# A two-layer hybrid decoder trunk in float32 on one core: rotary tables advanced inside the value phases and gate paths, head 0's values one step later, the last row tile in two column groups

## The chip, the cores and the metric

The kernel runs on one core of a Trainium2 chip. The metric is the device time of one execution in microseconds; the median of three runs is 2310.65 us. Five engines work side by side, each through its own queue in order: TensorE (PE, with its weight loads shown as PEld), VectorE (DVE), ScalarE (ACT), GpSimd (POOL) and SyncE (SP), which here issues the DMA transfers. An instruction waits for others by semaphores, and whatever stands behind a waiting instruction in its queue waits too.

## The reference

Two layers, then a final RMSNorm. Sequence 1024, width 1024, batch 1, everything in float32.

```python
for l in range(DEPTH):
    shift, scale, gate = jnp.split(c_act @ w_ada[l] + b_ada[l], 3, axis=-1)
    h = rmsnorm(x, norm_g[l]) * (1.0 + scale[:, None, :]) + shift[:, None, :]
    p = h @ w_in[l]
    mq, mk, mv, mo, mz, mi, mf, rq, rk, rv, rz = split_cols(p)
    qk = jax.nn.silu(causal_dwconv(jnp.concatenate([mq, mk], axis=-1), conv_w[l], conv_b[l]))
    ...
    y_m = jax.nn.sigmoid(mo) * head_layernorm(cell, gn_m[l], N_HEADS_MLSTM) * jax.nn.silu(mz)
    rq_h = rotary(rq.reshape(B, S, N_HEADS_RET, HD_R), positions)
    rk_h = rotary(rk.reshape(B, S, N_HEADS_RET, HD_R), positions)
    ret = retention_chunkwise(rq_h, rk_h, rv.reshape(B, S, N_HEADS_RET, HD_R))
    y_r = head_layernorm(ret, gn_r[l], N_HEADS_RET) * jax.nn.silu(rz)
    y = jnp.concatenate([y_m, y_r], axis=-1) @ w_out[l]
    x = x + gate[:, None, :] * y
return rmsnorm(x, final_g)
```

`cell` is the output of a chunkwise mLSTM with four heads of 256 columns, `ret` that of a chunkwise retention with four more. The rotary tables are cos and sin of position times 128 frequencies; they depend on the positions alone and are the same for both layers and for all retention heads.

## The kernel before

**Products.** Every float32 operand of a product is split into a rounded high part and a remainder (`split_to`, L620: the high part is cast on ACT in L621, the remainder subtracted in L622 on POOL or, where the caller says so, on DVE). `mm3` (L144) makes a product of three matmuls, high by high, high by low, low by high; its lines L145 to L147 carry most of TensorE's time.

**Heads.** The loop at L1268 goes over eight head groups, called heads 0 to 7 here: 0 to 3 are mLSTM, 4 to 7 retention. For a head come, in this order, the gate path (z and o columns, `gate_path`), the q and k columns (`qk_ml` with a convolution `conv_silu`, L630 to L645, or `qk_ret` with the rotary tables), the v columns (`v_path`, with the split of the values `v_split`, L596), and the attention. Columns of z, o, q and k are made by `proj_units`: a column block of 128 is two halves of 512 positions, each half two steps of 12 matmuls with 512 columns; after the second step `evac` empties the PSUM bank. `v_path` makes four chunks of two steps, each step 24 matmuls with 256 columns. PSUM has four banks under the tag `pp` for these products and four under `pa` for attention.

**Steps.** `run_units` (L140) calls `tick` after each step of such a generator. `tick` counts a clock and lets every generator that was put aside by `launch(gen, delay)` run on when it is due; `yield n` puts it off by n steps. So the attention of a head is written out in pieces between the projection steps of the heads after it. `attention` (L743) makes scores (L774), state updates (L807), values (L829) and their normalisation (L871) chunk by chunk; a state update runs from a product over L825 (cf, on DVE) to the cast cH (ACT, L621) and the remainder cL (DVE, L622), which the next values product (L845) needs. Head 0's attention is launched at the end of its turn with a delay of two steps (L1293), and so runs beside head 1's gate, q and k columns; those of heads 1 to 3 are launched ahead of their v columns with a delay of 7 or 4 (L1287).

**Order.** TensorE's instructions stand in the order in which the program writes them (L1107). For the start (L1109 to L1245) that holds for all engines. Everywhere else a scheduler decides the order on DVE, ACT, POOL and SP, and may draw an instruction that waits for little ahead of others that are written before it.

**Rotary tables.** `rotary_tables` (L374) makes the tables of the angle in four quarters of 256 positions. A quarter loads the positions by DMA (L381), needs 26 operations on DVE with 256 columns (L383 to L407) on three tiles of the tag `g`, and stores two results in DRAM (L410). The tag `g` has six buffers, which the z and o products of the gate path (L549 to L561) use too. In this kernel the generator is launched after head 1 of layer 0 with a delay of 14 steps (L1300). Head 3's attention loads the tables at its end (`load_rotary`, L735).

**Output product.** `out_units` (L975) multiplies the gated values by W_out. In the last layer a bank is a tile of 128 rows by 512 columns, and for the last half and the last 512 columns the final four of sixteen pieces are done row tile by row tile (`alone` is 4). `row_evac` (L1025) then loads the residual in four DMAs (L1030), multiplies by the gate (L1032), adds (L1033) and sums the squares on ACT (L1034); `final_rows` (L1090) turns the sum into a root (L1093, and L1094 on POOL) and `final_scale` (L1081) scales and stores the row (L1085, L1087, L1088).

Of the kernel before, what the change touches and what calls it, by code (L numbers as in the profile page):

```python
# [11 lines left out]
F32 = mybir.dt.float32  # L12
# [3 lines left out]
ALU = mybir.AluOpType  # L16
# [64 lines left out]
def tile_hybrid_trunk(ctx, tc, x, xt, c, positions, w_ada, b_ada, norm_g, w_in, conv_w, conv_b,  # L81
# [16 lines left out]
    def nm(s):  # L98
        uid[0] += 1
        return f"{s}_{uid[0]}"  # L100
# [39 lines left out]
    def run_units(gen):  # L140
        for _ in gen:
            tick()
# [231 lines left out]
    def rotary_tables():  # L374
        c1, c2, c3 = two_pi_split()
        tiles = [wt("g", 512, 6) for _ in range(3)]
        ang, turn, tmp, rnd, a1, pos = (t[:, i * CH:(i + 1) * CH] for t in tiles for i in range(2))
        a2 = ang
        for n in range(4):
            i, cs = n // 2, slice((n % 2) * CH, (n % 2 + 1) * CH)  # L380
            Q.dma_start(pos.bitcast(I32), positions[0:1, n * CH:(n + 1) * CH].to_broadcast([P, CH]))  # L381
            yield 2
            V.tensor_copy(ang, pos.bitcast(I32))  # L383
            V.tensor_scalar(ang, ang, kc[:, C_FREQ:C_FREQ + 1], None, ALU.mult)
            V.tensor_copy(a1.bitcast(F32R), ang)
            yield 1
            V.tensor_tensor(a2, ang, a1, ALU.subtract)
            V.tensor_scalar(turn, a1, c3, None, ALU.mult)
            yield 1
            V.scalar_tensor_tensor(turn, a2, c3, turn, ALU.mult, ALU.add)  # L390
            V.scalar_tensor_tensor(turn, a2, c2, turn, ALU.mult, ALU.add)
            yield 1
            for src, cc in ((a1, c2), (a2, c1), (a1, c1)):
                V.tensor_scalar(tmp, src, cc, None, ALU.mult)
                V.tensor_scalar(rnd, tmp, MAG_I, -MAG_I, ALU.add, ALU.add)
                yield 1
                V.tensor_tensor(tmp, tmp, rnd, ALU.subtract)
                V.tensor_tensor(turn, turn, tmp, ALU.add)
                yield 1
            parts = ((1, 0.0, tmp), (0, 0.25, a1))  # L400
            for which, sh, dst in parts:
                if sh:
                    V.tensor_scalar(turn, turn, sh, None, ALU.add)
                V.tensor_scalar(rnd, turn, MAG_I, -MAG_I, ALU.add, ALU.add)
                V.tensor_tensor(dst, turn, rnd, ALU.subtract)
                yield 1
                V.tensor_scalar(dst, dst, 0.49999994, -0.49999994, ALU.min, ALU.max)  # L407
            yield 2
            for which, sh, dst in parts:
                Q.dma_start(rdr[which][i][:, cs], dst)  # L410
            yield 2

    def v0_gates(l):
        gr = wt("wgr", KT * 8, 1)
# [328 lines left out]
    def attention(l, hg, gt, qT, kT, kt, vs, gp, rot):  # L743
# [230 lines left out]

    def out_units(l, half, cc, loads, evac, alone=0):  # L975
        banks = [ps_a() if cc else ps_p() for _ in range(4)]

        def product(k, piece, i):
            y, w = piece
            if l == 0:  # L980
                cs = slice(i * P, (i + 1) * P)
                mm3(banks[i], (w[0][:, cs], w[1][:, cs]), y, k == 0, k == 15)
            else:
                ts = slice(i * P, (i + 1) * P)
                mm3(banks[i], (y[0][:, ts], y[1][:, ts]), w, k == 0, k == 15)

        together = 16 - alone
        for k in range(together):
            piece = loads.take()
            for i in range(4):  # L990
                product(k, piece, i)
            yield
        pieces = [loads.take() for _ in range(alone)]
        for i in range(4):
            for k in range(together, 16):
                product(k, pieces[k - together], i)
            evac(half, cc, i, banks[i])
            if alone:
                yield

# [24 lines left out]
    def row_evac(gb, xnew, ss, done=None):  # L1025
        def evac(half, cc, tt, bank):
            xr = bt()
            src = xdr[half].rearrange("(g i) (b j) -> b i g j", i=32, j=32)[:, :, cc * 16:(cc + 1) * 16, :]
            for b in range(4):
                Q.dma_start(xr[b * 32:(b + 1) * 32, :].rearrange("i (g j) -> i g j", j=32), src[4 * tt + b])  # L1030
            tmp = wt("th", 512, 5)
            V.tensor_tensor(tmp, bank, gb[cc], ALU.mult)  # L1032
            V.tensor_tensor(xr, xr, tmp, ALU.add)  # L1033
            A.activation(tmp, xr, AF.Square, accum_out=ss[:, tt, cc:cc + 1])  # L1034
# [55 lines left out]
    def final_rows(xn, ss, half, fg, rows):  # L1090
        for tt in rows:
            s, rs = (cst.tile([P, 4], F32, tag=t, bufs=2, name=nm(t))[:, 0:1] for t in ("nrm", "nrmr"))
            V.tensor_scalar(s, ss[:, tt, 0:1], ss[:, tt, 1:2], EPS * D, ALU.add, ALU.add)  # L1093
            G.tensor_tensor(rs, s, mhalf[:, 0:1], ALU.pow)  # L1094
            final_scale(xn, rs, tt, half, fg)

    def final_later(xn, ss, half, fg):
        for tt in range(4):
            yield 2
            final_rows(xn, ss, half, fg, (tt,))  # L1100

    def gains_later(xn, fg):
        for tt in range(4):
# [57 lines left out]
    for l in range(DEPTH):  # L1161
# [103 lines left out]
        run_units(proj_units(load_w(w_in[l], zcol(1, 0), P), hT, z_evac(gp1, 0)))  # L1265
        gb = []
        gcol = gsh[0][:, 0, :]
        for hg in range(8):  # L1268
            ml = hg < 4
            if hg == 0:  # L1270
                rot = [[], []]
            if hg > 0:
                gp = gp1 if hg == 1 else [[None, None], [None, None]]
                run_units(gate_path(l, hg, hT, gp, 0, 1 if hg == 7 else 2, hg > 1))
            vs = []
            kt = [None] * NCH
            kT = [[None, None], [None, None]]
            qT = [[None] * NCH, [None] * NCH]
            if hg == 4:
                run_units(v_path(l, hg, hT, gt, vs))  # L1280
            for which, res in ((0, qT), (1, kT)):
                if ml:
                    run_units(qk_ml(l, hg, which, hT, gt, kt, res))
                else:
                    run_units(qk_ret(l, hg % 4, which, hT, kt, res, *rot))
            if 0 < hg < 4:
                launch(attention(l, hg, gt, qT, kT, kt, vs, gp, rot), 4 if hg == 3 else 7)  # L1287
            if hg not in (0, 4):
# [24 lines left out]
        for half in range(2):  # L1313
            if l < DEPTH - 1:
                xn, sq = [None] * KT, bt()
                keep = keep_rows(half, xn)
                evac = column_evac(gcol, xn, sq, keep)
                run_units(out_units(l, half, 0, loads, evac))
                run_units(out_units(l, half, 1, loads, evac, 2 if half else 0))
                launch(norm_later(l + 1, xn, sq, nhT, half, keep, (1, 2, 0) if half else (3, 3, 11)))  # L1320
                continue
            xn = [[None, None] for _ in range(4)]
            ss = new_ss()
            run_units(out_units(l, half, 0, loads, row_evac(gb, xn, ss)))
# [37 lines left out]
```

## Time and profile before

| | |
|---|---|
| median of three runs | 2310.65 us (2310.61 to 2311.62) |
| the profiled execution | 2310.2 us, of which the span from first to last instruction is 2308.5 us |
| matmuls | 12415 |
| mean granted TensorE clock | 0.997 |
| HBM read, written | 201.57 MB, 55.61 MB |

The profile is that of one execution. A row of its timeline has the start in us from the span's beginning, the duration in us, the engine, the line of the kernel, the operation, what it writes and reads (`out<-in`, buffer numbers left out), shapes, how many instructions were merged, and in brackets the idle time of the engine before it with what ended that wait. Matmuls are pipelined: one with 256 columns is shown with 0.28 us but the next starts about 0.12 us later. Idle time of an engine that is not the bottleneck costs nothing by itself.

### The profile page before, as it was taken

The page shows a single profiled execution, that of the slowest core. Times are in us where ns is not written, and L with a number is a line of the kernel's source. Part 1 is how long each engine was busy: PE and PEld are TensorE (multiplying, and loading weights), DVE is VectorE, ACT ScalarE, POOL GpSimd, SP SyncE. Part 2 cuts the span into 40 slices and gives each one's busy share as a digit, 9 for nine tenths or more (in the row PEclk, how much of TensorE's full clock was granted, in tenths as well). Part 3 has the DMA queues.
Part 4 walks back from the last instruction along what each step waited for, and adds up shares of the span by engine and source line. Part 5 has one row for each costly group of instructions (what it writes and reads, how often), then busy time and mean ns, then how long its engine had stood idle before and what let it go on. Part 6 is the DMA issues. An engine that isn't in the chain of part 4 may idle for free.

```text
span 2308.5 us, 34327 instructions
## 1 busy us (share of the span) xinstructions
PE 2273.0 (98%) x12415; PEld 1956.8 (85%) x12415; DVE 1337.9 (58%) x2823; ACT 919.3 (40%) x1768; POOL 830.7 (36%) x823
## 2 busy tenths in 40 slices
PE   7999999899999999999999999999999999999998
PEld 5888888789988888988888889888898888988886
DVE  7477669656555555585435676555563545557562
ACT  5535443444332323343544444344443323234342
POOL 1343433333244334224563433233334334341313
PEclk9999999999999999999999999999999999999999
DMA  8223233324433533385532323322223233436674
GB/s 257 80 64 96 74 80 85 78 74 117 119 100 102 149 94 83 113 261 201 174 107 70 81 72 81 82 74 74 75 71 94 76 91 88 124 81 212 182 240 120
DMA packets 360247, 259.45 MB, mean 112 GB/s; under 512 B 113267, under 2 KB 297339, under 8 KB 360077
## 3 DMA queue, kind: packets, MB, share of 16 engines
q1 hardware_dynamic: 360076, 257.26, 39.3%
q8 instruction: 97, 1.59, 0.3%
q14 instruction: 74, 0.60, 0.1%
HBM read 201.57 MB, written 55.61 MB: 111 GB/s over the span
## 4 chain that ended last, share of the span: by engine, by line
PE 91%; DVE 4%; DMA 2%; issue 1%; ACT 1%; POOL 0%; SPq 0%; POOLq 0%; ACTq 0%; DVEq 0%
PE pp L145 23%; PE pp L146 23%; PE pp L147 23%; PE pa L147 5%; PE pa L146 5%; PE pa L145 5%; PE pa L845 3%; PE pa L772 2%; DMA b<-in_w_ada_dram 1%; DVE acc L639 1%; DMA b<-in_x_dram 1%; PE pp L1178 0%; PE pp L1181 0%; PE pp L1179 0%; DVE acc L644 0%
## 5 line engine op out<-in xcount | busy, mean ns | idle before, releaser
L145 PE MATMUL pp<-b,wH 128*128 128x512 f32 x1824 | 721.1, 395 | 0.3 <-DVE g L550 0.3
L146 PE MATMUL pp<-b,wH 128*128 128x512 f32 x1824 | 718.1, 394 | 0.0
L147 PE MATMUL pp<-b,wL 128*128 128x512 f32 x1824 | 718.0, 394 | 0.0
L622 POOL TENSOR_TENSOR wL<-raw,wH 128x512 fp32r<-128x512 f32 x338 | 453.8, 1350 | 551.4 <-ACT wH L621 480.1
L147 PEld LDWEIGHTS pp<-b,wL 128*128 128x128 f32 x1824 | 342.6, 188 | 81.3
L145 PEld LDWEIGHTS pp<-b,wH 128*128 128x128 f32 x1824 | 342.8, 188 | 73.0 <-DVE g L550 0.8
L146 PEld LDWEIGHTS pp<-b,wH 128*128 128x128 f32 x1824 | 342.8, 188 | 72.3 <-issue 0.2
L621 ACT CAST wH<-raw 128x512 fp32r<-128x512 f32 x402 | 245.8, 617 | 324.0 <-PE pp L146 124.4
L145 PE MATMUL pp<-wH,b 128*128 128x256 f32 (+1 forms) x1024 | 302.8, 296 | 6.4 <-DVE acc L641 6.1
L147 PE MATMUL pp<-wH,b 128*128 128x256 f32 (+1 forms) x1024 | 302.6, 296 | 0.0
L146 PE MATMUL pp<-wL,b 128*128 128x256 f32 (+1 forms) x1024 | 302.5, 295 | 0.0
L622 POOL TENSOR_TENSOR b<-acc,b 128x256 fp32r<-128x256 f32 (+1 forms) x192 | 176.6, 940 | 303.6 <-ACT b L621 288.6
L145 PEld LDWEIGHTS pp<-wH,b 128*128 128x128 f32 x1024 | 193.4, 189 | 12.9 <-issue 6.3
L146 PEld LDWEIGHTS pp<-wL,b 128*128 128x128 f32 x1024 | 193.3, 189 | 5.8
L147 PEld LDWEIGHTS pp<-wH,b 128*128 128x128 f32 x1024 | 193.2, 189 | 5.7
L639 DVE SCALAR_TENSOR_TENSOR acc<-pp,cols,acc 128x511 f32<-128x511 f32 (+2 forms) x192 | 142.4, 742 | 39.3 <-ACT acc L634 37.3
L621 ACT CAST b<-acc 128x256 fp32r<-128x256 f32 (+1 forms) x192 | 83.7, 476 | 178.9 <-DVE acc L716 128.8
L622 POOL TENSOR_TENSOR sL<-th,sH 128x256 fp32r<-128x256 f32 (+1 forms) x62 | 57.4, 925 | 200.8 <-ACT sH L621 140.1
L643 ACT ACTIVATE th<-acc 128x512 f32<-128x512 f32 x64 | 40.5, 632 | 154.6 <-DVE acc L641 79.6
L621 ACT CAST cH<-cf 128x516 fp32r<-128x516 f32 (+1 forms) x80 | 49.7, 622 | 104.8 <-DVE va L893 57.8
L622 DVE TENSOR_TENSOR wL<-raw,wH 128x512 fp32r<-128x512 f32 x64 | 44.6, 699 | 51.3 <-ACT wH L621 48.8
L146 PE MATMUL pa<-b,b 128*128 128x256 f32 (+1 forms) x256 | 72.2, 282 | 0.0
(288 smaller groups left out, 3661.2 us busy)
## 6 DMA issues: line engine op xcount, KB each, us to landing
raw<-in_w_in_dram SPq DMA_DIRECT2D x274, 256.0 KB
raw<-in_w_out_dram SPq DMA_DIRECT2D x128, 256.0 KB
gdr<-g SPq DMA_DIRECT2D x64, 256.0 KB
ndr<-zt SPq DMA_DIRECT2D x128, 128.0 KB
raw<-in_w_ada_dram SPq DMA_DIRECT2D x64, 256.0 KB
g<-gdr SPq DMA_DIRECT2D x64, 256.0 KB
acc<-ndr SPq DMA_DIRECT2D x64, 256.0 KB
acc<-kdr SPq DMA_DIRECT2D x192, 64.0 KB
```

Of the source, the lines that this page charges most:

```text
L145: PE.matmul(o, lt[0], rt[0], start=start, stop=False)
L146: PE.matmul(o, lt[0], rt[1], start=False, stop=False)
L147: PE.matmul(o, lt[1], rt[0], start=False, stop=stop)
L621: A.copy(dst[0], src)
L622: eng.tensor_tensor(dst[1], src, f(dst[0]), ALU.subtract)
L639: V.scalar_tensor_tensor(acc[:, d:], pt[:, 0:HALF - d], wcol, acc[:, d:], ALU.mult, ALU.add)
L643: A.activation(th, acc, AF.Tanh, scale=0.5)
L772: PE.matmul(pd, kk[i][:, o:o + P], qd, start=dt == 0 and i == 0, stop=dt == 1 and i == 1)
L845: PE.matmul(pi[:, 0:W], qq[:, i * CH + tt * P:i * CH + (tt + 1) * P], state[part][:, dt, 0:W], start=part + dt + i == 0, stop=ml and part ...
```

## The change

There are three edits. Line numbers of the profile are those of the kernel before.

The tables: every wait of `rotary_tables` becomes single steps (a quarter has 15), the launch behind head 1 goes, and `run_beside` runs the generator by hand. In layer 0 it takes two of its steps after each step of `v_path` of heads 1, 2 and 3, and one after every second step of the gate path of heads 2 and 3; what is left after head 3's values follows there.

Head 0's values: the wait behind its second scores grows from 2 steps to 3, in both layers.

The last row tile: for the last half and last 512 columns of the last layer, the fourth row tile is made in two banks of 256 columns, first with the pieces that all row tiles share, then one column group after the other. `row_evac` multiplies, adds and squares it in two parts and adds the two sums. `final_last` computes each row's root as its squares are known, and scales row 2 after row 3's root instead of after its own.

```diff
     def rotary_tables():
...
             Q.dma_start(pos.bitcast(I32), positions[0:1, n * CH:(n + 1) * CH].to_broadcast([P, CH]))
-            yield 2
+            yield
+            yield
...
-            yield 2
+            yield
             for which, sh, dst in parts:
                 Q.dma_start(rdr[which][i][:, cs], dst)
-            yield 2
+            yield
+
+    def run_beside(gen, other, steps):
+        for n, _ in enumerate(gen):
+            for _ in range(steps[n % len(steps)]):
+                next(other, None)
+            tick()
...
         scores(1)
-        yield 2 if hg == 0 else 1
+        yield 3 if hg == 0 else 1
...
         banks = [ps_a() if cc else ps_p() for _ in range(4)]
-
-        def product(k, piece, i):
+        tail = (banks[3], ps_p()) if alone == 4 else None
+
+        def product(k, piece, i, parts=(0, 1)):
             y, w = piece
-            if l == 0:
+            if tail and i == 3:
+                ts = slice(i * P, (i + 1) * P)
+                for n in parts:
+                    mm3(tail[n][:, 0:CH], (y[0][:, ts], y[1][:, ts]), [x[:, n * CH:(n + 1) * CH] for x in w],
+                        k == 0, k == 15)
+            elif l == 0:
...
-            for k in range(together, 16):
-                product(k, pieces[k - together], i)
-            evac(half, cc, i, banks[i])
+            for parts in ((0,), (1,)) if tail and i == 3 else ((0, 1),):
+                for k in range(together, 16):
+                    product(k, pieces[k - together], i, parts)
+            evac(half, cc, i, tail if tail and i == 3 else banks[i])
...
-            V.tensor_tensor(tmp, bank, gb[cc], ALU.mult)
-            V.tensor_tensor(xr, xr, tmp, ALU.add)
-            A.activation(tmp, xr, AF.Square, accum_out=ss[:, tt, cc:cc + 1])
             xnew[tt][cc] = xr
+            if isinstance(bank, tuple):
+                s2 = wt("sm1", 4, 2)
+                for n in range(2):
+                    cs = slice(n * CH, (n + 1) * CH)
+                    V.tensor_tensor(tmp[:, cs], bank[n][:, 0:CH], gb[cc][:, cs], ALU.mult)
+                    V.tensor_tensor(xr[:, cs], xr[:, cs], tmp[:, cs], ALU.add)
+                    A.activation(tmp[:, cs], xr[:, cs], AF.Square, accum_out=s2[:, n:n + 1])
+                V.tensor_tensor(ss[:, tt, cc:cc + 1], s2[:, 0:1], s2[:, 1:2], ALU.add)
+            else:
+                V.tensor_tensor(tmp, bank, gb[cc], ALU.mult)
+                V.tensor_tensor(xr, xr, tmp, ALU.add)
+                A.activation(tmp, xr, AF.Square, accum_out=ss[:, tt, cc:cc + 1])
             if done:
-                done((tt,))
+                done(tt)
...
+    def final_root(ss, tt):
+        s, rs = (cst.tile([P, 4], F32, tag=t, bufs=2, name=nm(t))[:, 0:1] for t in ("nrm", "nrmr"))
+        V.tensor_scalar(s, ss[:, tt, 0:1], ss[:, tt, 1:2], EPS * D, ALU.add, ALU.add)
+        G.tensor_tensor(rs, s, mhalf[:, 0:1], ALU.pow)
+        return rs
+
+    def final_last(xn, ss, half, fg):
+        roots = {}
+
+        def done(tt):
+            roots[tt] = final_root(ss, tt)
+            for row in {0: (0,), 1: (1,), 2: (), 3: (2, 3)}[tt]:
+                final_scale(xn, roots[row], row, half, fg)
+        return done
...
+        tables = rotary_tables()
         for hg in range(8):
...
-                run_units(gate_path(l, hg, hT, gp, 0, 1 if hg == 7 else 2, hg > 1))
+                side = tables if l == 0 and 1 < hg < 4 else iter(())
+                run_beside(gate_path(l, hg, hT, gp, 0, 1 if hg == 7 else 2, hg > 1), side, (0, 1))
...
-                run_units(v_path(l, hg, hT, gt, vs))
+                side = tables if l == 0 and hg < 4 else iter(())
+                run_beside(v_path(l, hg, hT, gt, vs), side, (2,))
+                if hg == 3:
+                    for _ in side:
+                        tick()
...
-            if hg == 1 and l == 0:
-                launch(rotary_tables(), 14)
...
-                last = row_evac(gb, xn, ss, lambda rows: final_rows(xn, ss, 1, fg, rows))
+                last = row_evac(gb, xn, ss, final_last(xn, ss, 1, fg))
                 run_units(out_units(l, half, 1, loads, last, 4))
```

More of the change, by code (lines that the diff above doesn't have):

```diff
@@ L385, in rotary_tables @@
             V.tensor_copy(a1.bitcast(F32R), ang)
-            yield 1
+            yield
             V.tensor_tensor(a2, ang, a1, ALU.subtract)
             V.tensor_scalar(turn, a1, c3, None, ALU.mult)
-            yield 1
+            yield
             V.scalar_tensor_tensor(turn, a2, c3, turn, ALU.mult, ALU.add)
             V.scalar_tensor_tensor(turn, a2, c2, turn, ALU.mult, ALU.add)
-            yield 1
+            yield
             for src, cc in ((a1, c2), (a2, c1), (a1, c1)):
@@ L395, in rotary_tables @@
                 V.tensor_scalar(rnd, tmp, MAG_I, -MAG_I, ALU.add, ALU.add)
-                yield 1
+                yield
                 V.tensor_tensor(tmp, tmp, rnd, ALU.subtract)
                 V.tensor_tensor(turn, turn, tmp, ALU.add)
-                yield 1
+                yield
             parts = ((1, 0.0, tmp), (0, 0.25, a1))
@@ L405, in rotary_tables @@
                 V.tensor_tensor(dst, turn, rnd, ALU.subtract)
-                yield 1
+                yield
                 V.tensor_scalar(dst, dst, 0.49999994, -0.49999994, ALU.min, ALU.max)
-            yield 2
+            yield
             for which, sh, dst in parts:
                 Q.dma_start(rdr[which][i][:, cs], dst)
-            yield 2
+            yield
+    def run_beside(gen, other, steps):
[3 more added lines that the diff above has]
+            tick()
     def v0_gates(l):
@@ L1088, in final_scale @@
             Q.dma_start(out[row * P:(row + 1) * P, cc * 512:(cc + 1) * 512], xn[tt][cc])
[L1090 to L1095, printed above, removed]
+    def final_root(ss, tt):
[10 more added lines that the diff above has]
+        return done
     def final_later(xn, ss, half, fg):
@@ L1099, in final_later @@
             yield 2
-            final_rows(xn, ss, half, fg, (tt,))
+            final_scale(xn, final_root(ss, tt), tt, half, fg)
     def gains_later(xn, fg):
```

## The prediction

> **What bounds the kernel now.** The page first: TensorE is busy for nearly the whole span, so only what lengthens or shortens its row of matmuls, and the few us around it, can count.
>
> ```profile
> span 2308.5 us, 34327 instructions
> PE 2273.0 (98%) x12415; PEld 1956.8 (85%) x12415; DVE 1337.9 (58%) x2823; ACT 919.3 (40%) x1768; POOL 830.7 (36%) x823
> ```
>
> Then the waits of TensorE. Columns: who waits, for whom, us in total, times, longest. Both rows are VectorE (DVE) coming late.
>
> ```profile
> PE pp L145 <- DVE acc L641: 6.1, 1, 6.1
> ...
> PE pa L147 <- DVE sL L622: 1.2, 2, 0.6
> ```
>
> The timeline has the 6.1 us in head 2's v phase, first on TensorE and then on DVE.
>
> ```profile
> 406.84 0.28 PE L147 MATMUL pp<-wH,b 128*128 128x256 f32 x1
> 413.25 0.55 PE L145 MATMUL pp<-wH,b 128*128 128x256 f32 x1 [6.13 <-DVE acc L641]
> ```
>
> ```profile
> 404.56 0.29 DVE L385 CAST g<-g 128x256 fp32r<-128x256 f32 x1 [1.81 <-DMA rdr<-g]
> ...
> 410.58 0.29 DVE L404 TENSOR_SCALAR g<-g 128x256 f32<-128x256 f32 x1
> 410.79 0.74 DVE L639 SCALAR_TENSOR_TENSOR acc<-pp,cols,acc 128x511 f32<-128x511 f32 x1
> ```
>
> From 404.56 to 410.79 DVE works off rotary tables (L383 to L407, `g<-g`) with the convolution L639/L641 queued behind them; that convolution frees the PSUM bank which the next v product needs. Last, windows: busy us of PE, PEld, DVE, ACT, POOL (instructions), then the granted clock, DMA share, GB/s.
>
> ```profile
> 333.00:417.00 84.00, 77.87 (x428) 67.69 (x427) 76.38 (x189) 28.27 (x53) 26.64 (x24) 0.96 0.29 80
> ...
> 389.92:420.45 30.53, 24.40 (x193) 24.22 (x192) 27.09 (x66) 8.97 (x18) 7.17 (x6) 0.89 0.28 76
> 1527.03:1549.71 22.68, 22.68 (x194) 22.68 (x192) 8.31 (x18) 7.83 (x15) 5.01 (x4) 1.00 0.30 76
> 413.20:416.40 3.20, 3.15 (x15) 3.18 (x16) 3.13 (x9) 2.30 (x5) 0.97 (x1) 0.50 0.08 27
> ```
>
> The second row is the disturbed v phase, the third the same phase in layer 1, which has no tables: 7.85 us apart. That is the wait and, by the last row, 3.2 us at clock 0.50 after it. In the first row, the stretch that holds all the tables, DVE left only 84 - 76.38 = 7.6 us unused.
>
> **The change part by part.** *Tables, what is removed.* If they leave head 2's second half, the 7.85 us go. The price of the tables themselves (busy on tile g in that stretch, and two of their forms, min/median/max ns):
>
> ```profile
> 333.00:417.00 84.00, 0.00 (x0) 0.00 (x0) 46.16 (x106) 0.00 (x0) 0.96 0.29 80
> ```
>
> ```profile
> L394 DVE TENSOR_SCALAR g<-g x12: 252/288/1393, 337.9 to 409.0; 128x256 f32<-128x256 f32 x12
> ...
> L397 DVE TENSOR_TENSOR g<-g x12: 408/416/426, 340.4 to 409.7; 128x256 f32<-128x256 f32 x12
> ...
> L560 DVE SCALAR_TENSOR_TENSOR g<-th,g x2: 683/684/684, 338.8 to 350.1; 128x512 f32<-128x512 f32 x2
> ```
>
> Two of the 106 are gate products (L560), so the tables are 104 operations in 44.8 us. Without the outliers, 60 one-input operations at 0.288 and 44 others at 0.416 would be 35.6 us: the low bound.
>
> *Where they go.* The text hangs them on the v phases of heads 1 to 3, but only TensorE's order is written out; DVE's is the scheduler's. In the changed kernel's built DVE order the first table operation stands right behind head 0's first normalisation (192 us in this trace), 80 of the 104 stand ahead of the last convolution of head 1's keys, 21 more ahead of head 1's first scores, and the last three around its second scores. Nothing is left for heads 2 and 3: the tables only move up by some 140 us, into head 0's attention and head 1's projections.
>
> ```profile
> 192.00:271.00 79.00, 79.00 (x435) 68.21 (x434) 56.69 (x134) 38.63 (x79) 31.34 (x36) 1.00 0.28 74
> 271.00:294.00 23.00, 23.00 (x166) 21.62 (x165) 12.31 (x32) 10.82 (x22) 6.81 (x6) 1.00 0.40 99
> ```
>
> There DVE has 69.0 us of its own work in 102. With 44.8 it would be 113.8, and if it again leaves 9% unused (7.6 of 84, so 9.3 of 102) it needs 123.1: 21.1 us too many. Waits of its own are in that 9%: the cast L385 of each quarter waits for the quarter before to be stored (1.81 us at 404.56), and behind it now stand head 1's key convolutions. How late may it be? The bank of head 1's last key convolution and its next user:
>
> ```profile
> 270.94 0.20 DVE L641 SCALAR_TENSOR_TENSOR acc<-halo,cols,acc 128x3 f32<-128x3 f32 x1
> ```
>
> ```profile
> 278.81 0.28 PE L145 MATMUL pp<-wH,b 128*128 128x256 f32 x1
> ```
>
> 278.8 - 271.1 = 7.7 us. What goes beyond that stops TensorE: 21.1 - 7.7 = 13.4 us, in pieces, in head 0's attention, in head 1's v phase and in head 2's first gate units. The bounds: all 21 at the top; at the bottom 1.9 us, a wait which the order alone makes. In the new order the multiply of head 1's first scores (L786) stands ahead of the value splits (L673, L608) that free the bank for the gate product directly behind those scores:
>
> ```profile
> 291.21 1.11 PE L772 MATMUL pa<-b,b 128*128 128x256 f32 x8
> 292.15 0.40 PE L145 MATMUL pp<-b,wH 128*128 128x512 f32 x1
> ```
>
> ```profile
> 288.46 0.47 DVE L673 SCALAR_TENSOR_TENSOR b<-acc,wd,b 128x256 fp32r<-128x256 f32 x1
> 288.86 0.47 DVE L608 SCALAR_TENSOR_TENSOR b<-pp,eul,b 128x256 fp32r<-128x256 f32 x1
> ...
> 291.56 0.41 DVE L786 TENSOR_TENSOR th<-pa,dm 128x256 f32<-128x256 f32 x1
> ```
>
> L786 can't start before 291.56, then come two L673 and three L608 at about 0.4 each and two short casts: 294.0, against 292.15. I take 13.4, near the row it is most like: at the density of 333 to 417 DVE already stopped TensorE for 6.1.
>
> What the Trainium skill's page "SBUF — State Buffer", section "Who interferes with whom", adds is that GpSimd and a VectorE operation in a two-port mode lock each other out for a whole instruction; L394's 252 to 1393 ns agrees. By that rule the 9.2 us over the medians would grow with POOL's share (31.34 of 79 here, 26.64 of 84 there), an estimate of 47 us for the tables and 2.3 us more in the sum.
>
> The twelve table DMAs go onto SP's queue between weight loads in the same stretch; a store waits for its table and holds the loads behind it, covered by head 1's v weights being issued tens of us before use. That costs nothing; without the cover it would add to the same lag. The tables hold three of the six g buffers through head 2's gate path as the text has it; its four products turn over on the other three, whose stores have two projection halves (11 us, 48 matmuls at 0.23) to land. I cost it at nothing; without that cover a product waits one half, 5.6 us. The waits that become single steps cost no instruction.
>
> *Head 0's values one step later, in both layers.* Twelve projection matmuls now stand ahead of values(0), so its 0.6 us wait goes twice: -1.2. But head 0's whole attention shifts by one step against the projections: each state update now falls into the step that also runs a convolution, and in DVE's new order three L639 (and three L641) and an L644 stand between the update and cL, the split state that TensorE needs. Layer 1, without tables, shows the slack:
>
> ```profile
> 1354.84 0.69 DVE L622 TENSOR_TENSOR cL<-cf,cH 128x516 fp32r<-128x516 f32 x1 [2.10 <-ACT cH L621]
> ...
> 1362.25 1.20 DVE L622 TENSOR_TENSOR cL<-cf,cH 128x516 fp32r<-128x516 f32 x1 [0.36 <-ACT cH L621]
> 1363.45 0.75 DVE L639 SCALAR_TENSOR_TENSOR acc<-pp,cols,acc 128x511 f32<-128x511 f32 x1
> ...
> 1365.99 0.20 DVE L641 SCALAR_TENSOR_TENSOR acc<-halo,cols,acc 128x3 f32<-128x3 f32 x1
> ...
> 1366.95 0.69 DVE L644 SCALAR_TENSOR_TENSOR acc<-th,acc 128x512 f32<-128x512 f32 x1
> ```
>
> ```profile
> 1356.85 0.41 PE L845 MATMUL pa<-cL,b 128*128 128x258 f32 x2
> ...
> 1364.23 0.40 PE L845 MATMUL pa<-cL,b 128*128 128x258 f32 x2
> ```
>
> Slack: 1356.85 - 1355.53 = 1.3 and 1364.23 - 1363.45 = 0.8; a third update is taken like the first. Put in: 2.7 us for the first kind (no halo columns), 3.3 for the second (1363.45 to 1366.11 and 0.6 for L644). If all of it delays cL: 1.4 + 2.5 + 1.4 = 5.3 us; if DVE does it while it would idle (2.10 us idle in the first row): 0. I take half, 2.7, for layer 1. Layer 0 has the same insertions, inside the 13.4.
>
> *Last row tile in two groups.* 48 matmuls of 512 columns become 96 of 256: from the v phase 22.68/192 = 118 ns each, 11.3 us, against 48 at 0.23 (starts below) = 11.1: +0.2 on TensorE. Behind the last matmul:
>
> ```profile
> 2298.09 0.40 PE L146 MATMUL pa<-wL,b 128*128 128x512 f32 x1
> 2298.32 0.39 PE L147 MATMUL pa<-wH,b 128*128 128x512 f32 x1
> ```
>
> ```profile
> 2301.70 0.69 DVE L1033 TENSOR_TENSOR b<-b,th 128x512 f32<-128x512 f32 x1 [0.71 <-DMA b<-xdr]
> ...
> 2304.05 0.75 DVE L1085 SCALAR_TENSOR_TENSOR b<-b,nrmr,b 128x512 f32<-128x512 f32 x1 [0.66 <-POOL nrmr L1094]
> ```
>
> ```profile
> 2298.83 0.46 SPq L1030 DMA_DIRECT2D b<-xdr  x1
> ```
>
> ```profile
> 2302.42 0.63 ACT L1034 ACTIVATE th<-b 128x512 f32<-128x512 f32 x1 [1.47 <-DVE b L1033]
> ```
>
> The multiply is not what ends last: the add L1033 waits for the last piece of the residual, issued at 2298.83 behind row 1's output. SP's order at the tail is the same in both kernels, and row 2's scale, which the text puts behind row 3's root, keeps its place in DVE's order; so both half-adds start together at that landing; the first square may save 0.3, a second square, its accumulator read and the extra add cost up to 0.7. I take +0.3, with TensorE +0.5 (-0.1 to +0.9).
>
> *Clock.* The wait at 406.84 cost more than itself: in the clock 0.50 row 15 matmuls take 3.2 us, 0.213 each instead of 0.118, 1.4 us in all. One such piece: +1.4 (0 to 4.2 for three).
>
> **Sum**, against this execution's 2310.2 us (span 2308.5 and 1.7 around it; the median of the runs, 2310.65, is 0.45 above, which I neglect): -7.85 - 1.2 + 13.4 + 2.7 + 0.5 + 1.4 = +8.95, so 2319.
>
> **Rivals.**
> *The tables hide (the other side).* The 102 us of head 0 and 1 have 33 us of idle DVE and the bank 7.7 of slack; speaking against it is the 9% that was never usable. If the tables take under 31 us (0.30 each: 69 + 31 + 9.3 - 102 = 7.3, inside the slack) no stop is left but perhaps layer 1's: -9.05 + 0.5 + 2.7 to -9.05 + 0.5, 2302 to 2304.4; say 2303, faster.
> *The tables run at their medians,* 35.6 us: 69 + 35.6 + 9.3 - 102 - 7.7 = 4.2 of stops: -9.05 + 4.2 + 2.7 + 0.5 = -1.65, 2308.5, no measurable change. For it: most rows stand at the median; against: POOL is busier there.
> *Every delay lands and the clock halves three times:* 13.4, 5.3 and 4.2 give +14.4, 2324.6; with 21 instead of 13.4, 2332. For it: several stops follow each other closely. The skill's page "TensorE: Matmul & The Clock Gate", section "What's actually happening", has the clock halve after an idle window of about 3.4 us. By that rule stops under 3.4 us cost no clock, and the sum would be 2317.8; the 0.50 row after a 6.13 us wait agrees, and no row here tests a shorter one.
>
> **How the numbers follow.** Forecast 0.50, tables hidden 0.13, medians 0.22, everything lands 0.15. The forecast's own range is 2315 to 2323. The range of 8 in 10 takes in the median case and most of the last: 2306 to 2330. 0.2% is 4.6 us, what a measurement of this kernel can tell from no change: faster 0.13, same 0.22, slower 0.65.
>
> **What would show it.** Right: table rows between 190 and 300 us; head 2's v phase at 22.7; new TensorE waits for cL or cH (L622, L621) in head 0 of both layers, for L641 in head 1's v phase, for L608 in head 2's first gate unit; values(0) without a wait; the tail still ended by the residual's DMA. Wrong: TensorE unbroken from 190 to 310, or layer 1's head 0 as long as before.

## The result and the profile after

The changed kernel takes 2322.28 us in the median of 6 runs (2321.51 to 2324.30), the kernel before 2311.12 us on the same chip (2310.61 to 2311.62): ratio 1.0050, 95% interval [1.0038, 1.0063], so slower by 11.2 us. The profiled execution took 2321.98 us, 11.8 more than the one of before. From about L600 on the line numbers are seven higher than before (L622 is L629, L845 is L852), those of the tail some twenty.

The page of the changed kernel, then its waits of TensorE, the rows that are new:

```profile
span 2320.0 us, 34430 instructions
PE 2278.9 (98%) x12463; PEld 1962.6 (85%) x12463; DVE 1346.2 (58%) x2826; ACT 920.7 (40%) x1770; POOL 829.8 (36%) x823
```

```profile
PE pp L145 <- DVE b L615: 4.4, 1, 4.4
PE pa L852 <- ACT cH L628: 4.2, 4, 2.0
PE pa L852 <- DVE cL L629: 3.5, 4, 1.6
...
PE pa L145 <- DVE th L794: 0.4, 1, 0.4
```

The rows of 6.1 us (for the convolution) and of 1.2 us (for sL) are gone, and 12.5 us stand in their place. Where they lie, in the timeline of TensorE of the changed kernel:

```profile
224.22 0.74 PE L852 MATMUL pa<-cH,b 128*128 128x258 f32 x4 [1.97 <-ACT cH L628]
226.55 0.80 PE L852 MATMUL pa<-cL,b 128*128 128x258 f32 x2 [1.59 <-DVE cL L629]
236.71 0.75 PE L852 MATMUL pa<-cH,b 128*128 128x258 f32 x4 [0.47 <-ACT cH L628]
238.31 0.50 PE L852 MATMUL pa<-cL,b 128*128 128x258 f32 x2 [0.86 <-DVE cL L629]
305.00 0.79 PE L145 MATMUL pp<-b,wH 128*128 128x512 f32 x1 [4.38 <-DVE b L615]
1366.49 0.74 PE L852 MATMUL pa<-cH,b 128*128 128x258 f32 x4 [0.77 <-ACT cH L628]
1368.02 0.51 PE L852 MATMUL pa<-cL,b 128*128 128x258 f32 x2 [0.79 <-DVE cL L629]
1377.75 0.75 PE L852 MATMUL pa<-cH,b 128*128 128x258 f32 x4 [1.02 <-ACT cH L628]
1378.75 0.51 PE L852 MATMUL pa<-cL,b 128*128 128x258 f32 x2 [0.25 <-DVE cL L629]
```

Head 0's values wait for their state in both layers, and head 2's first gate product waits for the splits of head 1's values. With 0.45 for `th` at 216 us, layer 0 has 9.7 us of waits, layer 1 has 2.8. The windows of the changed kernel, first the new home of the tables, then head 2's v phase:

```profile
190.00:303.00 113.00, 105.29 (x599) 91.66 (x597) 103.00 (x256) 47.47 (x98) 41.94 (x43) 0.97 0.32 84
```

```profile
405.56:428.24 22.68, 22.68 (x193) 22.68 (x192) 8.31 (x18) 7.89 (x15) 5.00 (x4) 1.00 0.29 77
```

```profile
185.00:305.00 120.00, 0.00 (x0) 0.00 (x0) 49.69 (x106) 0.00 (x0) 0.97 0.34 89
```

Head 2's v phase is at 22.68 us, as long as in layer 1. VectorE is busy for 103.00 of the 113 us from 190 to 303. In the third row, that of the tiles g alone, are all 104 operations of the tables and two gate products. VectorE ahead of the 4.38 us wait, and GpSimd (POOL) in the same stretch:

```profile
291.79 1.52 DVE L391 SCALAR_TENSOR_TENSOR g<-g 128x256 f32<-128x256 f32 x1
...
302.12 0.28 DVE L404 TENSOR_SCALAR g<-g 128x256 f32<-128x256 f32 x1
302.32 0.42 DVE L793 TENSOR_TENSOR th<-pa,dm 128x256 f32<-128x256 f32 x1
302.66 0.87 DVE L680 SCALAR_TENSOR_TENSOR b<-acc,wd,b 128x256 fp32r<-128x256 f32 x2
303.44 0.48 DVE L615 SCALAR_TENSOR_TENSOR b<-pp,eul,b 128x256 fp32r<-128x256 f32 x1
```

```profile
291.59 5.60 POOL L629 TENSOR_TENSOR wL<-raw,wH 128x512 fp32r<-128x512 f32 x4 [3.19 <-ACT wH L628]
```

From 290.3 to 302.4 table operations follow each other, with one value split among them near the start; the multiply of head 1's scores L793 and the value split L615, for which TensorE waits, come directly behind. Four of them, from 291.79 to 297.5, take 1.39 to 1.52 us each, 5.9 together, while GpSimd works through four subtractions; at their shortest in this trace the same lines take 0.25 to 0.41, 1.5 together. The scores that L793 reads start at 299.53, so by the distance in the trace of before (291.56 - 291.21) it could have started at 299.9 instead of 302.32: 2.4 of the 4.38 us are the tables' lag, and the rest is about the 1.9 that the order alone makes.

Shifts of whole stages tell the rest. The table gives, for the first matmul of a stage, how much later it starts in a trace than in the trace of before (us; the two traces' start times subtracted). The columns behind the first are experiments that are described below:

| stage | changed | step only (a1) | tables only (a2) | changed with wait 4 (c3) | wait 4 only (a4) | b2 |
|---|---|---|---|---|---|---|
| head 1, v phase (261.8 before) | +8.3 | +5.8 | +6.8 | +6.2 | -1.2 | -0.9 |
| head 2, v phase (389.9) | +15.6 | +5.9 | +13.7 | +10.3 | -1.3 | -0.1 |
| right behind it (420.5) | +7.8 | +7.1 | +5.8 | +2.5 | -1.0 | -7.9 |
| late in layer 0 (967.3) | +7.7 | +7.1 | +5.5 | +1.9 | -1.6 | -2.3 |
| layer 1, head 1, v phase (1398.7) | +11.9 | +12.6 | +5.2 | +0.3 | -3.2 | -3.9 |
| last matmul (2298.3) | +11.9 | +12.6 | +5.1 | -0.2 | -4.2 | -4.7 |

In the changed kernel 15.6 us are lost up to head 2's v phase and 7.85 come back in it; layer 1's head 0 loses 4.2 more. The waits do not fill these losses: 15.6 less 0.4 that stand there from the start is 15.2, against 9.7 of waits, less the 0.6 that values(0) no longer waits. The other 6.1 us, and 2.0 in layer 1, stand in no wait row. The windows show the greater part of them as clock. First windows of 3.4 us of the changed kernel:

```profile
235.70:239.10 3.40, 2.07 (x13) 1.44 (x12) 3.40 (x9) 1.88 (x5) 1.60 (x2) 1.00 0.06 11
239.10:242.50 3.40, 3.40 (x19) 2.89 (x18) 3.22 (x11) 0.88 (x3) 0.00 (x0) 1.00 0.02 5
1365.50:1368.90 3.40, 1.84 (x12) 1.42 (x12) 3.24 (x6) 2.08 (x5) 2.90 (x3) 1.00 0.11 19
1368.90:1372.30 3.40, 3.40 (x12) 2.92 (x12) 1.93 (x4) 0.55 (x2) 2.30 (x3) 0.50 0.19 63
```

```profile
303.90:310.80 6.90, 5.80 (x15) 4.64 (x16) 6.29 (x20) 3.18 (x7) 1.04 (x1) 0.51 0.14 38
225.40:232.30 6.90, 5.75 (x19) 5.08 (x20) 6.30 (x16) 2.15 (x4) 3.83 (x4) 0.51 0.29 77
```

After the two stops of 0.77 and 0.79 us at 1366 to 1368 the next 3.4 us run at clock 0.50 and hold 12 matmuls. After the stops of 0.47 and 0.86 at 236 to 238 the next 3.4 us keep clock 1.00 and hold 19. In layer 0 two stretches of 6.9 us are halved. What the clock cost can be estimated from the distance between the starts of two matmuls, which in the trace of before is 0.118 us with 256 columns, 0.120 with 258 and 0.232 with 512 (medians). What the matmuls of the three halved stretches took beyond that, the waits left out, is 2.7, 2.7 and 1.5 us: 6.9 us for the clock. The last 1.3 us or so stand at the stops themselves: a wait in brackets counts from the shown end of the matmul before it, 0.28 us after its start, where the next one could have started after 0.12. That makes 0.16 us more for each of the ten stops, less the two of values(0) that are gone.

The tail of the changed kernel, SP and VectorE:

```profile
2310.47 0.45 SPq L1044 DMA_DIRECT2D b<-xdr  x1
```

```profile
2313.03 0.76 DVE L1052 TENSOR_TENSOR b<-b,th 128x256 f32<-128x256 f32 x2 [0.41 <-DMA b<-xdr]
2314.42 0.16 DVE L1054 TENSOR_TENSOR ss<-sm 128x1 f32<-128x1 f32 x1 [0.64 <-ACT th L1053]
...
2315.55 0.75 DVE L1108 SCALAR_TENSOR_TENSOR b<-b,nrmr,b 128x512 f32<-128x512 f32 x1 [0.72 <-POOL nrmr L1116]
```

Both half-adds (one row of x2) start when the residual's last piece has landed. The span ends 11.5 us later than before and the last matmul 11.85, so the stretch behind it is 0.35 shorter.

### The profile page after: what moved, and what is told of

Its sections match the earlier page's. It is cut to its first block, busy times and chain, and to the rows that moved or that the text cites. A ratio compares the mean times of both kernels' runs of the same rounds, so it can differ in the third digit from the quotient of the medians.

```text
span 2320.0 us, 34430 instructions
## 1 busy us (share of the span) xinstructions
PE 2278.9 (98%) x12463; PEld 1962.6 (85%) x12463; DVE 1346.2 (58%) x2826; ACT 920.7 (40%) x1770; POOL 829.8 (36%) x823
## 4 chain that ended last, share of the span: by engine, by line
PE 54%; DVE 1%; issue 1%; DMA 0%; POOL 0%; ACT 0%; POOLq 0%; SPq 0%; DVEq 0%; ACTq 0%
PE pp L145 13%; PE pp L146 13%; PE pp L147 13%; PE pa L147 3%; PE pa L145 3%; PE pa L146 3%; PE pa L852 2%; PE pa L779 1%; PE pp L1209 0%; PE pp L1212 0%; PE pp L1210 0%; DMA b<-xdr 0%; PE pa L1212 0%; PE pa L1210 0%; PE pa L1209 0%
## 5 line engine op out<-in xcount | busy, mean ns | idle before, releaser
L629 POOL TENSOR_TENSOR wL<-raw,wH 128x512 fp32r<-128x512 f32 x338 | 451.8, 1345 | 544.8 <-ACT wH L628 491.7
L145 PE MATMUL pp<-wH,b 128*128 128x256 f32 (+1 forms) x1040 | 306.2, 294 | 0.3 <-DVE g L557 0.3
L147 PE MATMUL pp<-wH,b 128*128 128x256 f32 (+1 forms) x1040 | 306.4, 295 | 0.0
L629 POOL TENSOR_TENSOR b<-acc,b 128x256 fp32r<-128x256 f32 (+1 forms) x192 | 178.3, 949 | 297.1 <-ACT b L628 285.8
L145 PEld LDWEIGHTS pp<-wH,b 128*128 128x128 f32 x1040 | 195.7, 188 | 6.5 <-DVE g L557 0.7
L147 PEld LDWEIGHTS pp<-wH,b 128*128 128x128 f32 x1040 | 195.6, 188 | 5.7
L629 POOL TENSOR_TENSOR sL<-th,sH 128x256 fp32r<-128x256 f32 (+1 forms) x62 | 55.9, 902 | 222.3 <-ACT sH L628 169.2
L629 DVE TENSOR_TENSOR wL<-raw,wH 128x512 fp32r<-128x512 f32 x64 | 44.5, 698 | 51.9 <-ACT wH L628 49.6
```

Source lines behind the costliest of these rows:

```text
L145: PE.matmul(o, lt[0], rt[0], start=start, stop=False)
L147: PE.matmul(o, lt[1], rt[0], start=False, stop=stop)
L629: eng.tensor_tensor(dst[1], src, f(dst[0]), ALU.subtract)
```

## The experiments

Each kernel is the kernel before with the edit shown, unless it says otherwise. Ratios are to the kernel before on the same chip, with 95% intervals.

**The three parts alone.** a1, the step:

```diff
-        yield 2 if hg == 0 else 1
+        yield 3 if hg == 0 else 1
```

> The kernel before with one edit alone: the wait behind head 0's second scores is 3 steps instead of 2. Theory (one step later puts each state update of head 0 into a step that also runs a convolution on DVE, so cL comes late): both layers lose what layer 1 lost in the changed kernel, 4.2 us each with the clock's part, so about 2311 + 8.4 = 2319.5 us, with waits of TensorE for cH and cL in head 0 of both layers; the 6.1 us wait in head 2's v phase stays. Rival (the packed tables are the whole loss, the step only takes its 0.6 us wait away twice): 2310 us.

Measured: 2322.55 us, ratio 1.0046 [1.0033, 1.0058], 3 us over the theory. a2 takes the first edit of the change (the tables) and nothing else; a3 the last one (the row tile).

> The kernel before with the table edit alone. Theory (the tables are drawn into head 0 and head 1 and overload DVE there, but without the step the updates keep their slack): layer 0 costs 15.6 us as in the changed kernel less the 4.2 that the step makes, and head 2's v phase gives 7.85 back: about 2311 + 3.5 = 2314.6 us; layer 1 as before. Rival (tables are the whole loss): 2323.5 us. Rival (the step is the whole loss): 2303 us.

> The kernel before with the edit of the last row tile alone. Theory (the residual's last piece ends the tail, not the multiply): no difference within 0.5 us, 2311 us. Rival (the two column groups take half a row's multiply, add and square off the end): 2310 us or less, with the last add no longer released by the residual's DMA.

Measured: a2 2315.94 us, ratio 1.0021 [1.0012, 1.0030]; a3 2311.74 us, ratio 1.0001 [0.9992, 1.0010]. The one step alone costs as much as the whole change. VectorE in layer 1 of the changed kernel, where no tables run, shows how:

```profile
1373.51 0.44 DVE L832 SCALAR_TENSOR_TENSOR cf<-cf,wd,pa 128x258 f32<-128x258 f32 x1
1373.87 0.74 DVE L646 SCALAR_TENSOR_TENSOR acc<-pp,cols,acc 128x511 f32<-128x511 f32 x1
...
1376.11 0.21 DVE L648 SCALAR_TENSOR_TENSOR acc<-halo,cols,acc 128x3 f32<-128x3 f32 x1
...
1376.57 0.47 DVE L832 SCALAR_TENSOR_TENSOR cf<-cf,wd,pa 128x258 f32<-128x258 f32 x1
```

The state is updated in two halves (L832), and a whole convolution, 1373.87 to 1376.3, stands between them. So the cast cH on ACT comes late, and cL behind it. This is the third update, for which TensorE waits 1.02 and 0.25 us at 1377 to 1379; for the second, at 1366 to 1368, cL itself also took long, 1.49 us where the third took 0.68. In a1 the second update stops TensorE alike, and the third once, for longer:

```profile
1366.00 0.75 PE L845 MATMUL pa<-cH,b 128*128 128x258 f32 x4 [0.80 <-ACT cH L621]
1367.54 0.52 PE L845 MATMUL pa<-cL,b 128*128 128x258 f32 x2 [0.78 <-DVE cL L622]
1377.28 1.13 PE L845 MATMUL pa<-cH,b 128*128 128x258 f32 x4 [2.58 <-ACT cH L621]
```

a2 has the stop of head 2's gate product without the step, so that stop is the tables'; and it has a state's cL late in head 0:

```profile
232.51 0.73 PE L852 MATMUL pa<-cL,b 128*128 128x258 f32 x2 [2.07 <-DVE cL L629]
```

```profile
304.13 0.67 PE L145 MATMUL pp<-b,wH 128*128 128x512 f32 x1 [5.02 <-DVE b L615]
```

The parts do not add: 11.5, 4.9 and 0.7 make 17, together they take 11.2. In layer 0, up to head 1's v phase, the step shifts by 5.8 and the tables by 6.8, both by 8.3: probably VectorE catches up on the one while TensorE stands for the other, which no run tests apart. In layer 1, where no table runs, the step loses 5.5 us alone and 4.2 in the changed kernel, and the traces put this down to the clock. VectorE does the same work in the same order in both, some 0.5 us apart (cL of the third update at 1377.55 in a1 and 1378.02). In the changed kernel the clock is halved behind the stops at 1366 to 1368, so TensorE comes later to the third update and waits 1.27 us less for it than the 2.58 of a1. In a1 the clock stays full behind the first two stops and is halved behind the third, where nothing hides it. The last section has the windows.

**Is it late, or is it odd?** A projection half is two steps of 12 matmuls and ends in an evacuation, so a wait of 2, 4 and 3, 5 steps differ in which step an update meets. a4 has a wait of 4, c1 of 5.

```diff
-        yield 2 if hg == 0 else 1
+        yield 4 if hg == 0 else 1
```

> The kernel before with the wait behind head 0's second scores at 4 steps instead of 2. Theory (what costs is that an update falls into a step with a convolution; two steps later it falls between them again): the 0.6 us wait of values(0) is gone in both layers and no cL wait comes, about 2310 us. Rival (any delay costs, since head 0's attention then lies deeper in head 1's convolutions): as slow as one step later or slower, 2319 us or more.

> Head 0's wait of 2 made 5, nothing else; tables and tail as before. Theory (even and odd: a projection half is two steps, so an odd wait lays every state update of head 0 into the step that ends with an evacuation and a convolution): waits for cH or cL of 2 to 4 us in head 0 of both layers and 2319 to 2323 us. Rival (only the 2 and 3 are too early, later is better): no wait in head 0, at most 2308 us.

Measured: a4 2306.86 us, ratio 0.9982 [0.9973, 0.9990]; c1 2316.46 us, ratio 1.0023 [1.0014, 1.0032]. Odd waits stop TensorE for cH or cL in both layers, even ones do not; "later is better" falls with c1, though c1 loses less than the theory asked. In c1, too, rows of the convolution stand between the halves of an update (L639 between 1369.70 and 1372.43); in a4 no more than its last row does (L644 between 1362.75 and 1363.86), and TensorE does not wait. a4 is 3 us better than expected. Of its 4.2 us of gain 1.2 are the two waits of values(0); most of the rest stands in no wait row, and its cause stays open. One place stays in a4, and it is the one the tables make:

```profile
412.12 0.55 PE L145 MATMUL pp<-wH,b 128*128 128x256 f32 x1 [6.25 <-DVE acc L641]
```

c3 is the changed kernel with its 3 made 4:

```diff
-        yield 3 if hg == 0 else 1
+        yield 4 if hg == 0 else 1
```

> The changed kernel with its wait of 3 made 4, nothing else: tables drawn ahead into heads 0 and 1 as there. Theory (the step's part and the tables' part are two stops, the first by the odd step, the second by an overfull VectorE): layer 1's head 0 gets back 4 us, layer 0 keeps what the tables alone did there (shift of 6 to 7 us up to head 1's v phase, the gate wait of 4 to 5 us behind it): 2311 to 2314 us. Rival (tables alone keep head 0 as late as in the changed kernel whatever the step): 2317 us or more.

Measured: 2310.34 us, ratio 0.9997 [0.9989, 1.0006], 0.7 below the 2311 to 2314 expected. One step more takes 11.9 us off the changed kernel, half of it in layer 1 (the shift from late in layer 0 to layer 1's head 1 is -1.6 instead of +4.2). What is left in layer 0 is the tables':

```profile
245.11 0.80 PE L852 MATMUL pa<-cL,b 128*128 128x258 f32 x2 [2.19 <-DVE cL L629]
```

```profile
300.73 0.50 PE L145 MATMUL pp<-b,wH 128*128 128x512 f32 x1 [2.21 <-DVE b L615]
```

**Tables where the text puts them.** In b1 the table steps are taken as in the change, but may not be drawn ahead: what a step issues is ordered behind the last VectorE operation of the unit beside it (the anchor is set in `v_split`, in the gate product and in the convolution). Wait 2, tail as before. b2 is b1 with a wait of 4.

```diff
     def run_beside(gen, other, steps):
         for n, _ in enumerate(gen):
-            for _ in range(steps[n % len(steps)]):
-                next(other, None)
+            with tc.issue_after(anchor[0].ins):
+                for _ in range(steps[n % len(steps)]):
+                    next(other, None)
             tick()
```

> The table edit alone, but each piece of the tables on DVE is queued behind the last DVE operation of the unit beside which it is written (a value split, a convolution or a gate product), so that the scheduler cannot draw it ahead; head 0's step and the last row tile as before. Theory (the loss of the tables is where the scheduler put them, not their price): the tables stand in the v phases and gate paths of heads 1 to 3, head 2's v phase takes 22.7 us, no new wait: 2311 - 7.85 = 2303 us. Rival (DVE has no room for them beside the value splits either): new waits of TensorE for L608 or L641 in the v phases, 2307 us or more.

> As the kernel with the gated tables, and head 0's wait at 4 steps. Theory: another 1.2 us off if two steps later is free, 2302 us. Rival (any delay of head 0 costs): slower than the gated tables alone, 2306 us or more.

Measured: b1 2308.66 us, ratio 0.9986 [0.9977, 0.9996], by its time the rival's, though not with the waits that the rival names; b2 2304.01 us, ratio 0.9968 [0.9956, 0.9981], between theory and rival, and the lowest median of this study. Apart from the 0.6 us of values(0) in b1 nothing stops in head 0 or for L641 any more, and head 2's v phase gives its 7.85 back. But 4.3 (b1) and 5.5 us (b2) are lost right behind it; TensorE in b1:

```profile
426.33 0.39 PE L146 MATMUL pa<-b,sH 128*128 128x258 f32 x1 [1.15 <-ACT sH L630]
428.26 0.57 PE L148 MATMUL pa<-b,sL 128*128 128x258 f32 x1 [1.43 <-POOL sL L631]
```

Head 2's first scores come late. In b1 table operations stand among them, so c2 (b2 with other step counts) keeps those free:

```diff
-    run_beside(gate_path(l, hg, hT, gp, 0, 1 if hg == 7 else 2, hg > 1), side, (0, 1))
+    run_beside(gate_path(l, hg, hT, gp, 0, 1 if hg == 7 else 2, hg > 1), side, (0, 0, 0, 0, 0, 0, 0, 1))
-    run_beside(v_path(l, hg, hT, gt, vs), side, (2,))
+    run_beside(v_path(l, hg, hT, gt, vs), side, (5, 5, 5, 0, 0, 0, 0, 0))
```

with the last entry standing for all later steps.

> The gated tables with a wait of 4, but in a v phase the table steps come five at a time behind its first three steps and none behind the other five, and in the gate paths of heads 2 and 3 only from the eighth step on, so that none stands among a head's first scores. Theory (what b1 and b2 lost was pieces between head 2's first scores, 2.6 us of waits for sH and sL and 1.7 of clock): those waits go, 2299 to 2301 us. Rival (VectorE has no room for the tables in heads 1 to 3 wherever they stand): 2303 us or more, with waits elsewhere.

Measured: 2305.31 us, ratio 0.9974 [0.9964, 0.9985]: the theory falls, with b2's waits at the same place. VectorE and TensorE in c2:

```profile
422.05 0.41 DVE L400 TENSOR_TENSOR g<-g,g 128x256 f32<-128x256 f32 x1
422.38 0.47 DVE L617 SCALAR_TENSOR_TENSOR b<-pp,eul,b 128x256 fp32r<-128x256 f32 x1
...
422.91 0.41 DVE L795 TENSOR_TENSOR th<-pa,dm 128x256 f32<-128x256 f32 x1
```

```profile
424.84 0.39 PE L146 MATMUL pa<-b,sH 128*128 128x258 f32 x1 [1.29 <-ACT sH L630]
```

No table operation is among the scores' multiplies, and TensorE waits for sH as in b2 (1.29 us against 1.15). The tables stand among the value splits L617, and the multiply L795 is queued behind those. d1 tests this: no table step in head 2's v phase, denser ones elsewhere.

```diff
-    run_beside(gate_path(l, hg, hT, gp, 0, 1 if hg == 7 else 2, hg > 1), side, (0, 1))
+    run_beside(gate_path(l, hg, hT, gp, 0, 1 if hg == 7 else 2, hg > 1), side, (0, 0, 0, 0, 0, 0, 0, 1) if hg == 2 else (0, 0, 1))
-    run_beside(v_path(l, hg, hT, gt, vs), side, (2,))
+    run_beside(v_path(l, hg, hT, gt, vs), side, (5, 5, 5, 5, 0, 0, 0, 0) if hg == 1 else
+               (0,) if hg == 2 else (3, 3, 3, 3, 0, 0, 0, 0))
```

> Gated tables and a wait of 4 again, with no table step in head 2's v phase at all: five at a time behind the first four steps of head 1's v phase, one a step in the gate path of head 2 from the eighth step and of head 3 from the third, three at a time behind the first four steps of head 3's v phase. Theory (b1, b2 and c2 were stopped because the tables made head 2's last value splits late, and the multiply of its first scores stands behind those): the waits for sH and sL at 424 to 428 us and the halved clock behind them go, 2299 to 2301 us. Rival (those waits come from the shorter v phase itself, in which VectorE is no longer given 6 us to catch up): they stay without any table work near, 2304 us or more.

Measured: 2316.55 us, ratio 1.0024 [1.0015, 1.0033]. The place behaves as the theory said: no wait stands between 420 and 430 us. The total is some 16 us over the expectation, for two stops elsewhere. The first comes in head 1, where the tables now stand among the value splits and the scores' multiplies; 5.2 us are lost from there to head 2's v phase (shift from -1.1 to +4.2). The second comes behind head 3's v phase, and 10.2 us are lost in it (shift from -4.0 at that phase to +6.1 at 740 us). TensorE in heads 1 and 3 of d1, and the windows around the second stop:

```profile
296.60 0.39 PE L146 MATMUL pa<-b,sH 128*128 128x258 f32 x1 [2.56 <-ACT sH L630]
```

```profile
554.93 1.23 PE L854 MATMUL pa<-cH,b 128*128 128x258 f32 x4 [3.99 <-ACT cH L630]
```

```profile
550.90:554.30 3.40, 0.04 (x1) 0.00 (x0) 3.40 (x15) 3.22 (x11) 0.78 (x3) 1.00 0.29 108
554.30:564.50 10.20, 7.64 (x29) 6.75 (x30) 9.61 (x35) 3.76 (x9) 1.52 (x2) 0.50 0.04 14
```

A stop of nearly a whole window is followed by 10.2 us at half clock, with 0.8 and 1.1 us of further waits in them. This second stop is not the same as the others. d1's step counts use up 55 of the 60 table steps; the five that are left are taken behind head 3's values, each with a `tick` and with no projection step beside it. So head 3's attention is written in one piece: between the v phase and the next projection stand 54 of its matmuls in d1, and 9 in the kernel before. The first matmul of that projection, before and in d1:

```profile
552.26 0.39 PE L145 MATMUL pp<-b,wH 128*128 128x512 f32 x1
```

```profile
563.13 0.63 PE L146 MATMUL pp<-b,wH 128*128 128x512 f32 x1
```

The edit has thus changed TensorE's own order as well, and how much of these 10.2 us the tables alone would have cost is not shown. Spread thinly, as in b2, the tables cost 5 us (2304.0 against a4's 2306.9 less head 2's 7.85); a looser packing that also spares head 2 was not tried.

## Why the prediction was right, and which of its steps were not

The forecast of 2319 was 3.3 us under the median, with the right sign and the right cause, VectorE coming late for TensorE. Term by term:

- *Head 2's v phase, -7.85.* As worked out: the shift falls from 15.64 to 7.79 across it, 7.85.
- *values(0), -1.2.* Both waits for sL are gone.
- *The tables move up into heads 0 and 1.* Right; the order on VectorE decided, not the text. They took 48.3 us (49.69 less two gate products of 0.68) where I put 44.8, nearer to the 47 that the lock between VectorE and GpSimd gave as an estimate (the Trainium skill, "SBUF — State Buffer", section "Who interferes with whom"). VectorE again left 9% unused: 113.00 - 103.00 = 10.0 us.
- *Layer 0's stops, +13.4.* Measured 9.7 us of waits. Right in kind, mis-sized, and its cause was half of it: the insertions by the step, which I counted as "inside the 13.4", are a stop of their own (a1: 5.8 us without the tables having moved; c3 against the changed kernel: 5.8 us in layer 0, 7.7 less 1.9). The expected wait for L641 in head 1's v phase did not come: that phase starts 8.3 us late and ends 8.3 us late. The lag came out at head 2's first gate product, 4.38 instead of the 1.9 that the order alone makes.
- *Layer 1's head 0, +2.7.* Measured 2.8 us of waits, which is partly luck: 2.7 was half of a bound. I put the convolution between the update and cL; for the third update it stands between the update's two halves, so that cH is late too.
- *Last row tile, +0.5.* a3's ratio is 1.0001 with an interval around 1; the residual's landing still ends the tail. The multiplies of two halves, the second square and the extra add cost nothing that can be told from no change.
- *Clock, +1.4.* This is the step that failed: "One such piece: +1.4 (0 to 4.2 for three)". There were three places, with 17.2 us at half clock (6.9, 6.9, 3.4) instead of one with 3.2. They cost 6.9 us by the distances between matmuls. By the rule I cited from the Trainium skill, page "TensorE: Matmul & The Clock Gate", section "What's actually happening", stops under 3.4 us should have cost no clock. The rows of 1365.50 and 1368.90 say otherwise: 1.56 us idle in a window, half clock in the next.

Too much on the stops (13.4 for 9.7) and too little on the clock (1.4 for 6.9) nearly cancelled: that the total came so near is luck, the sign and most of the places are not. Of the rivals, "every delay lands and the clock halves three times" was right about the three halvings, though it priced them at 4.2, and wrong about the delays; the tables at their medians (35.6 us) are excluded by the 48.3; "the tables hide" is what b1 and b2 approach, when the tables are kept from being drawn ahead.

## What to carry to other kernels

On an engine whose order a scheduler writes, moving work in the text moves it only if something ties it there: work that waits for nothing is drawn to the front, and b1 needed an explicit order to keep it back. A piece of attention that is fitted between projection steps has a phase, and one step off it (3 or 5 instead of 2 or 4) put a convolution into a state update and cost 5 to 12 us. Price a stop of TensorE by what follows it as well: here the halved clock added about half of the waits' own 12.5 us.

## What the runs showed of the hardware

In the traces the clock changes only on a grid of windows of 3.41 us, which lies differently in each execution. A window of the changed kernel in which TensorE was busy for 1.84 us (idle 1.56) was followed by one at clock 0.50, one with 2.07 busy (idle 1.33) by one at 1.00. It need not be one stop: the 1.56 us are two, of 0.77 and 0.79. In a1 the same pair, 0.80 and 0.78, has a window's edge inside the second stop, and the clock stays full:

```profile
1363.80:1367.20 3.40, 2.15 (x11) 1.33 (x9) 3.28 (x9) 2.80 (x6) 1.70 (x2) 1.00 0.02 5
1367.20:1370.60 3.40, 3.06 (x18) 2.76 (x19) 2.51 (x5) 0.00 (x0) 3.10 (x4) 1.00 0.28 77
```

Over the windows at full clock of all twelve traces, from 100 to 2290 us, the fifteen with 2.26 us or more of idle time were all followed by half clock, and none with 1.33 or less. Between them the idle time alone does not decide: with 1.55 to 1.73 us four were followed by half clock (the changed kernel, b2, c1, c3), and with 1.51 to 1.86 four by full clock (a1, c3 and two of a2). What tells these apart is open; two of the latter, 1.77 in a2 and 1.86 in a1, are the beginning of a long stop, and the clock was halved one window later. Where a halved window itself held 0.85 us or more of idle time, which it did ten times, the next one was halved too: so the two stops of layer 0, which reach 1.06 and 1.12 us into a halved window, cost two windows each.
